# Own buffers for PSUM copies, a last norm updated on one engine, and attention heads scored in pairs, in a two-block fp32 network on one Trainium2 core

## The chip, the cores and the metric

The kernel runs on one core of a Trainium2 chip. The metric is the device time of one execution in microseconds; lower is better.

## The reference

All data are fp32; the sequence is 512 tokens of width 1024. Cut to what matters here:

```python
def first_block(x, mem, ...):                       # two layers
    for layer in range(2):
        x = x + 0.5 * swiglu_ffn(rms_norm(x, g1), w_gu, w_down)          # d_ff 2816
        h = rms_norm(x, mix_norm)
        x = x + (even_mixer(h) if layer % 2 == 0 else odd_mixer(h))
        x = x + memory_cross_attention(rms_norm(x, gx), rms_norm(mem, gm), ...)
        x = x + 0.5 * swiglu_ffn(rms_norm(x, g2), w_gu, w_down)
# even_mixer: 8 banded heads (with sinks) + 8 stick-breaking heads, head size 64
# odd_mixer:  16 heads, three dilated windows merged into one score bias
# second block: index scores of 8 heads of 64 -> top-k mask, a gated recurrence,
#   16 attention heads of 64 under that mask, a merge with gates, then
x = x + rms_norm(h @ w_att_out, out_gain)           # its norm is the "last norm" below
x = x + swiglu_ffn(rms_norm(x, g3), w_gu, w_down)   # last feed-forward block
x = rms_norm(x, g4)
```

## The kernel before

Activations stand with features on the 128 partitions and the 512 tokens along the free axis, as eight blocks `X[0..7]`. Every fp32 operand is split into a high and a low part, and each product is three matmuls: high by high, high by low, low by high (`mm3`, L312 to L314). GH and GL are the split, gain-scaled inputs of the next stage; `block_done` makes them for one block (GH on ScalarE L580, GL on VectorE L581) and adds its squares for the next norm.

A feed-forward block computes its up products as seven half-size products instead of eight (`unit`). The weights of a product are combined, cast (L427, ScalarE) and reduced by the high part (L428, VectorE). Products collect in PSUM banks x, y and z. Three times in a unit a bank's content is kept for a later sum while the bank goes on collecting: `keep` (L477) copies it on ScalarE into a slot of the common pool of 38 (L184). The products need combined inputs of block k and block k+4 too, which `pair_done` (L398 to L406) makes, mostly on VectorE.

A head of the mixers (`head`, L911 to L977) takes three PSUM banks (two in the even mixer), writes 12 score matmuls over 64 rows (L927), adds the bias and takes the maximum (L931, VectorE), exponentiates with sums (L940, ScalarE), normalises (L951, GpSimd), transposes on TensorE (L962), copies out of PSUM in two parts (`evac`, L851 ScalarE and L852 VectorE) and multiplies by the values (L975 to L977). It is a generator: `drive` steps every active head once a tick and starts new heads and "fills" (projections, output products, gates) as lists of ticks written by hand say. Head h uses rows 0 to 63 of the array if h is even, 64 to 127 if odd. The index scores of the second block use the same row halves with `mm3`.

The last norm sits in the function that ends the second block's merge. It works in two halves of 256 tokens: `update` multiplies each of the eight blocks by the factor R (L1671), adds it to the residual (L1672) and calls `block_done`. The factor comes from sums of squares over the partitions on TensorE (L545), a reciprocal root on VectorE and ScalarE (L527 to L537), transposes back (L558) and a copy (L561). A tile scheduler places every instruction in its engine's queue, by when its inputs and buffers are there in its own estimate, so an edit can move instructions that it does not touch.

Of the kernel before, what the change touches and what calls it, by code (L numbers as in the profile page):

```python
# [114 lines left out]
class Slot:  # L115
# [12 lines left out]
    @property  # L128
    def f(self):
        return self._get(F32)  # L130
# [44 lines left out]
class Net:  # L175
    def __init__(self, ctx, tc, a):
        self.ctx, self.tc, self.nc, self.a = ctx, tc, tc.nc, a
        pool = lambda name, bufs, **k: ctx.enter_context(tc.tile_pool(name=name, bufs=bufs, **k))
        self.cp = pool("const", 1)
        self.wp = pool("weights", 1)  # L180
        self.tp = pool("temps", 2)
        self.sp = pool("small", 4)
        self.ps = pool("psum", 8, space=bass.MemoryType.PSUM)
        self.room = ctx.enter_context(tc.tile_pool(name="slots", bufs=38, reuse_waits="tile"))  # L184
        self.live = self.peak = 0
        self.listed = False
        self.n = 0
        self.scope = None
        self.phase("mix")
        self.setup()  # L190
# [240 lines left out]
    def unit(self, load, B, done):  # L431
# [42 lines left out]
        def keep(b, name):  # L474
            def go():
                s = kept[name] = self.get()
                nc.scalar.copy(s.f, banks[b])  # L477
            return go

        def out(which, b, name=None):  # L480
            def go():
                s = kept.pop(name, None)
                done(which, banks[b], s and s.f)
                if s:
                    self.put(s)
            return go
# [86 lines left out]

    def block_done(self, b, c=slice(0, S), apart=1):
# [335 lines left out]

    def head(self, lay, q, k, r0, bias, v, pair, second, sink=None, gap=1):  # L911


        nc = self.nc
        mm = nc.tensor.matmul
        rows = slice(r0, r0 + 64)
        sb = [self.bank() for _ in range(lay["n"])]
        pb = self.get(lay["n"])
        mx, nm, den, rd = (self.small(NT, t, 6) for t in ("mx", "nm", "den", "rd"))
        seen = set()  # L920
# [24 lines left out]
        for _ in range(gap - 1):  # L945
            yield
        nc.vector.reciprocal(rd, den)
# [38 lines left out]
    def even_mixer(self, rms, w, wout):  # L986
# [28 lines left out]

        def a_head(h):
            p = h // 2
            if h % 2 == 0:
                st["pa", p] = []
            bt = self.vbias(a["c_bias_a"][h], 256)  # L1020
            yield from self.head(self.LAY_A, st["q", p], st["k", h // 4], (h % 2) * 64,
                                 lambda i, wd: bt.f[:, 256 - wd:256],
                                 lambda j: self.vslice(st["v"], j, 128 * (h // 4) + (64 if h % 2 == 0 else 0)),
                                 st["pa", p], h % 2 == 1, sink=sinks[:, h:h + 1], gap=2)
            self.put(bt)
            if h % 2 == 1:
                OH[p], OL[p] = self.finish_pair(st["pa", p][0])
                self.put(*st["q", p])
            if h % 4 == 3:
                self.put(*st["k", h // 4])  # L1030

# [26 lines left out]
        def b_head(h):  # L1058
# [10 lines left out]
        B = lambda h: lambda: b_head(h)  # L1069
        A = lambda h: lambda: a_head(h)  # L1070
        f = lambda g, *x: lambda: g(*x)
# [10 lines left out]
            ([f(proj_b, 0, 3)], [B(5), A(0)]),  # L1082
            ([f(proj_b, 1, 3)], [A(1)]),
            ([f(proj_q, 1)], [B(6), B(7)]),
            ([], []),
            ([], []),
            ([], [A(2)]),
            ([], [A(3)]),
            ([outs[0]], [A(4)]),
            ([], [A(5)]),  # L1090
            ([outs[1]], [A(6)]),
            ([], [A(7)]),
            ([outs[2]], []),
# [92 lines left out]
    def odd_mixer(self, rms, w, wout):  # L1186
# [20 lines left out]

        def head(h):
            p = h // 2
            if h % 2 == 0:  # L1210
                st["po", p] = []
            bt = self.vbias(a["c_bias_o"][h], 512)
            yield from self.head(self.LAY_C, st[0, p], st[1, p], (h % 2) * 64,
                                 lambda i, wd: bt.f[:, 512 - wd:512],
                                 lambda j: self.vslice(st["v", p // 2], j, (p % 2) * 192 + (h % 2) * 64),
                                 st["po", p], h % 2 == 1, gap=2)
            self.put(bt)
            if h % 2 == 1:
                OH[p], OL[p] = self.finish_pair(st["po", p][0])
                self.put(*st[0, p], *st[1, p])  # L1220

        outs = self.out_units(wout, OH, OL, range(ND))
        H = lambda h: lambda: head(h)
# [271 lines left out]
    def index_scores(self, st, W, i):  # L1495
# [5 lines left out]
        if i == 0:  # L1501
# [3 lines left out]
            return  # L1505
        for h in range(8):
            if h == 4:
                yield
            ps = self.bank()[:, :wd]
            rows = slice((h % 2) * 64, (h % 2) * 64 + 64)  # L1510
            t = slice(i * P, (i + 1) * P)
            qh, ql = iq[h // 2]
            self.mm3(ps, qh.r[rows, t], ql.r[rows, t], ik[0].r[rows, :wd], ik[1].r[rows, :wd], True, True)
            rl = self.scratch()[:, :wd]
            nc.scalar.activation(rl, ps, AF.Relu)
            wc = self.iw[:, i * 8 + h:i * 8 + h + 1]
            if h == 0:
                nc.vector.tensor_scalar(o, rl, wc, None, OP.mult)
            else:
                nc.vector.scalar_tensor_tensor(o, rl, wc, o, OP.mult, OP.add)  # L1520
        nc.vector.tensor_add(o[:, wd - P:], o[:, wd - P:], self.caus)
# [114 lines left out]
    def out_norm(self, w, XH, XL, gname):  # L1636
# [152 lines left out]
    def second(self, out):  # L1789
# [95 lines left out]

        def head(h):
            p, g = h // 2, h // 4
            if h % 2 == 0:
                st["po", p] = []
            yield from self.head(self.LAY_C, Q[p], K[g], (h % 2) * 64, bias,  # L1890
                                 lambda j: self.vslice(V[g // 2], j, 128 * (g % 2) + (64 if h % 2 == 0 else 0)),
                                 st["po", p], h % 2 == 1, gap=2)
            if h % 2 == 1:
                OH[p], OL[p] = self.finish_pair(st["po", p][0])
                self.put(*Q[p])
            if h % 4 == 3:
                self.put(*K[g])
# [23 lines left out]

        H = lambda h: lambda: head(h)
        B = lambda b: lambda: merge_b(b)
# [3 lines left out]
        for h in range(16):  # L1927
            x = [q(h // 4 + 1)] if h % 4 == 0 and h < 12 else [G(h // 2)] if h % 2 else []
            ticks.append((x, [H(h)]))
        self.drive(ticks + [([B(0)], []), ([B(1)], [])])  # L1930
# [108 lines left out]
```

## Time and profile before

| | |
|---|---|
| three runs | 3272.19, 3276.24, 3276.51 us, median 3276.24 |
| the profiled execution | 3273.41 us, span of its instructions 3271.6 us |
| TensorE, VectorE, ScalarE, GpSimd busy | 3179.1, 2245.2, 1611.8, 372.0 us |
| granted clock of TensorE, mean over the span | 0.988 |

Device times compare whole runs; the profile shows where one execution spent its span. The 1.8 us between the profiled time and its span lie around the instructions.

### The profile page before, as it was taken

To read this page: it belongs to the slowest core of one execution; us is meant where nothing else is said; L and a number is where in the kernel's file an instruction comes from. 1 tells how busy PE (TensorE), PEld (TensorE's weight loads), DVE (VectorE), ACT (ScalarE), POOL (GpSimd) and SP (SyncE) were. 2 spreads that over 40 slices of the span, in tenths; PEclk is the share of its full clock that TensorE was granted. 3 is DMA by queue.
4 is the path that set the end of the run, shared out by engine and by line. 5 is a ranking of instruction groups with operands and counts; after the bars stand their busy time and mean duration, and the time that the engine had idled before them with its cause. 6 is when DMAs were issued, how large, how long until landed. Compare 5 with 4: busy or idle time off the path is not lost. (4 is left out here: it accounts for less than half of the span.)

```text
span 3271.6 us, 51295 instructions
## 1 busy us (share of the span) xinstructions
PE 3179.1 (97%) x20612; PEld 2863.6 (88%) x20612; DVE 2245.2 (69%) x3384; ACT 1611.8 (49%) x2687; POOL 372.0 (11%) x593
## 2 busy tenths in 40 slices
PE   7999999999999999999999999999998999989998
PEld 6999888898899989999998988999876888879887
DVE  8877656656777697865666457776689455477765
ACT  6544455555444364434555554444485366354444
POOL 1000122201000010001122010000322132210001
PEclk9999999999999999999999999999999999989999
DMA  4332211322233323322223322332322322413322
GB/s 157 101 104 84 86 57 52 123 92 86 84 103 101 98 94 105 97 83 88 85 80 114 104 84 73 109 101 73 107 65 88 106 65 72 155 39 104 104 90 65
DMA packets 104335, 300.82 MB, mean 92 GB/s; under 512 B 13856, under 2 KB 17440, under 8 KB 104096
## 3 DMA queue, kind: packets, MB, share of 16 engines
q1 hardware_dynamic: 94464, 287.74, 27.3%
q10 hardware_dynamic: 9632, 9.80, 1.0%
q8 instruction: 161, 2.64, 0.3%
q14 instruction: 78, 0.64, 0.1%
HBM read 291.21 MB, written 6.29 MB: 91 GB/s over the span
## 5 line engine op out<-in xcount | busy, mean ns | idle before, releaser
L312 PE MATMUL bank<-slot,whi 128*128 128x256 f32 (+1 forms) x2768 | 913.0, 331 | 18.5 <-ACT slot L477 11.3
L313 PE MATMUL bank<-slot,whi 128*128 128x256 f32 (+1 forms) x2768 | 910.5, 329 | 0.4 <-DVE slot L518 0.4
L314 PE MATMUL bank<-slot,wlo 128*128 128x256 f32 (+1 forms) x2768 | 910.4, 329 | 0.0
L427 ACT CAST whi<-fq 128x1024 fp32r<-128x1024 f32 x350 | 366.5, 1048 | 548.4 <-PE bank L313 461.8
L306 ACT CAST whi<-raw 128x1024 fp32r<-128x1024 f32 (+3 forms) x363 | 345.5, 953 | 523.7 <-PE bank L313 318.8
L312 PEld LDWEIGHTS bank<-slot,whi 128*128 128x128 f32 x2768 | 521.6, 189 | 75.7 <-ACT slot L477 15.8
L314 PEld LDWEIGHTS bank<-slot,wlo 128*128 128x128 f32 x2768 | 522.9, 189 | 51.5
L313 PEld LDWEIGHTS bank<-slot,whi 128*128 128x128 f32 x2768 | 521.5, 188 | 52.2 <-DVE slot L518 1.5
L312 PE MATMUL bank<-gh,whi 128*128 128x256 f32 (+1 forms) x1712 | 539.9, 316 | 22.2 <-ACT whi L352 8.5
L307 DVE TENSOR_TENSOR wlo<-raw,whi 128x1024 fp32r<-128x1024 f32 (+3 forms) x363 | 407.0, 1122 | 214.5 <-ACT whi L306 213.6
L314 PE MATMUL bank<-gh,wlo 128*128 128x256 f32 (+1 forms) x1712 | 536.4, 313 | 4.2 <-DVE wlo L353 2.8
L313 PE MATMUL bank<-gl,whi 128*128 128x256 f32 (+1 forms) x1712 | 537.3, 314 | 2.8 <-DVE gl L581 2.8
L428 DVE TENSOR_TENSOR wlo<-fq,whi 128x1024 fp32r<-128x1024 f32 x350 | 427.2, 1222 | 156.5 <-ACT whi L427 156.1
L312 PEld LDWEIGHTS bank<-gh,whi 128*128 128x128 f32 x1712 | 326.3, 191 | 49.9 <-ACT whi L427 9.7
L314 PEld LDWEIGHTS bank<-gh,wlo 128*128 128x128 f32 x1712 | 326.9, 191 | 26.0 <-DVE wlo L353 3.5
L313 PEld LDWEIGHTS bank<-gl,whi 128*128 128x128 f32 x1712 | 326.8, 191 | 26.0 <-DVE gl L581 4.3
L788 PE MATMUL bank<-whi,gh 128*128 128x256 f32 (+1 forms) x1056 | 301.8, 286 | 0.0
L789 PE MATMUL bank<-wlo,gh 128*128 128x256 f32 (+1 forms) x1056 | 298.9, 283 | 1.0 <-DVE wlo L307 0.9
L790 PE MATMUL bank<-whi,gl 128*128 128x256 f32 (+1 forms) x1056 | 298.9, 283 | 1.0 <-DVE gl L581 0.8
L172 POOL TENSOR_TENSOR sqacc<-sqacc,slot 128x512 f32<-128x512 f32 x62 | 98.3, 1585 | 924.8 <-ACT slot L168 884.3
L788 PEld LDWEIGHTS bank<-whi,gh 128*128 128x128 f32 x1056 | 199.8, 189 | 1.9 <-DVE slot L855 0.3
L789 PEld LDWEIGHTS bank<-wlo,gh 128*128 128x128 f32 x1056 | 199.9, 189 | 1.8 <-DVE wlo L307 1.6
(320 smaller groups left out, 4731.2 us busy)
## 6 DMA issues: line engine op xcount, KB each, us to landing
fq<-in_ffn_w_gu_dram SPq DMA_DIRECT2D x160, 512.0 KB, 3.3
raw<-in_ffn_w_down_dram SPq DMA_DIRECT2D x96, 384.0 KB, 3.0
raw<-in_w_in_dram SPq DMA_DIRECT2D x46, 512.0 KB, 3.4
raw<-in_xa_w_kv_dram SPq DMA_DIRECT2D x32, 512.0 KB, 3.4
raw<-in_od_w_in_dram SPq DMA_DIRECT2D x24, 512.0 KB, 3.8
raw<-in_w_ffn_down_dram SPq DMA_DIRECT2D x22, 512.0 KB, 3.5
fq<-in_w_ffn_gate_dram SPq DMA_DIRECT2D x40, 256.0 KB, 2.8
fq<-in_w_ffn_up_dram SPq DMA_DIRECT2D x40, 256.0 KB, 3.1
```

The costliest lines, as they stand in the source:

```text
L172: self.net.nc.gpsimd.tensor_add(self.parts[0], self.parts[0], sq)
L306: nc.scalar.copy(hi[:, :n], raw[:, :n])
L307: nc.vector.tensor_sub(lo[:, :n], raw[:, :n], hi[:, :n].bitcast(F32))
L312: mm(ps, wh, xh, start=start, stop=False, **k)
L313: mm(ps, wh, xl, start=False, stop=False, **k)
L314: mm(ps, wl, xh, start=False, stop=stop, **k)
L427: self.nc.scalar.copy(hi[:, :n], t[:, :n])
L428: self.nc.vector.tensor_sub(lo[:, :n], t[:, :n], hi[:, :n].bitcast(F32))
L788: mm(o, XH[k][:, t], wh, start=first, stop=False, skip_group_check=True)
L789: mm(o, XH[k][:, t], wl, start=False, stop=False, skip_group_check=True)
L790: mm(o, XL[k][:, t], wh, start=False, stop=last, skip_group_check=True)
```

## The change

It makes four edits. The common pool has 36 slots and not 38, and `keep` copies into two buffers of its own (`kept`). In the last norm all eight multiplications of a half are on VectorE (four were on GpSimd), and the combined inputs of all four pairs are made behind the last block of the second half, instead of as soon as both blocks of a pair are there. In the mixers and the second block, two heads with opposite row halves become one generator `heads`, whose 24 score matmuls alternate between the halves; the rest of each head follows as before, the second head's stages being a tick later than the first's from the normalisation on, and a pair starts every second tick. The index scores alternate in the same way.

```diff
-        self.room = ctx.enter_context(tc.tile_pool(name="slots", bufs=38, reuse_waits="tile"))
+        self.room = ctx.enter_context(tc.tile_pool(name="slots", bufs=36, reuse_waits="tile"))
...
-                s = kept[name] = self.get()
-                nc.scalar.copy(s.f, banks[b])
+                kept[name] = self.tp.tile([P, 512], F32, name=self.uid("kept"), tag="kept", bufs=2)
+                nc.scalar.copy(kept[name], banks[b])
...
-            if self.pairs is not None and (b + 4) % ND in self.there:
+            if pairs and self.pairs is not None and (b + 4) % ND in self.there:
                 self.pair_done(b % 4)
...
+    def heads(self, lay, q, k, biases, values, pair, sinks=(None, None)):
+        mm = self.nc.tensor.matmul
+        sb = [[], []]
         order = sorted(range(NT), key=lambda i: (lay["Q"][i][0], lay["Q"][i][1]))
         for i in order:
             b, off, w, k0 = lay["Q"][i]
-            o = sb[b][:, off:off + w]
+            new = b == len(sb[0])
+            if new:
+                for x in sb:
+                    x.append(self.bank())
             qs, ks = slice(i * P, (i + 1) * P), slice(k0, k0 + w)
             for z, (A, B) in enumerate(((0, 0), (0, 1), (1, 0))):
-                mm(o, q[A].r[rows, qs], k[B].r[rows, ks], start=z == 0 and b not in seen, stop=z == 2, skip_group_check=True)
-            seen.add(b)
+                for x in range(2):
+                    rows = slice(64 * x, 64 * x + 64)
+                    mm(sb[x][b][:, off:off + w], q[A].r[rows, qs], k[B].r[rows, ks], start=z == 0 and new, stop=z == 2,
+                       skip_group_check=True)
+        one, two = (self.head(lay, order, sb[x], biases[x], values[x], pair, x == 1, sinks[x]) for x in range(2))
+        next(one)
+        next(two)
+        yield
+        next(one)
+        yield
+        next(one)
+        next(two)
+        yield
+        next(one, None)
+        next(two)
+        yield
+        next(two, None)
...
-        ticks += [([fills[h]] if h in fills else [], [H(h)]) for h in range(16)]
+        ticks += [([fills[h]] if h in fills else [], [] if h % 2 else [H(h // 2)]) for h in range(16)]
...
-        for h in range(8):
-            if h == 4:
+        for p in range(4):
+            if p == 2:
                 yield
...
+            for z, (A, B) in enumerate(((0, 0), (0, 1), (1, 0))):
+                for x in range(2):
+                    rows = slice(64 * x, 64 * x + 64)
+                    mm(ps[x], iq[p][A].r[rows, t], ik[B].r[rows, :wd], start=z == 0, stop=z == 2)
...
-                (nc.gpsimd if b % 2 else nc.vector).tensor_mul(m, m, R)
+                nc.vector.tensor_mul(m, m, R)
                 nc.vector.scalar_tensor_tensor(self.X[b][:, c], m, self.col(gname, b), self.X[b][:, c], OP.mult, OP.add)
-                self.block_done(b, c, 4)
+                self.block_done(b, c, 4, False)
+            if z:
+                for k in range(4):
+                    self.pair_done(k)
```

Three places show what the scheduler makes of it. On TensorE, in the odd mixer, the 12 score matmuls of one head stood together, between a projection and transposes; one bank after the other:

```order
L927 MATMUL bank_16247<-slot_15754,slot_15842 128x512
L927 MATMUL bank_16247<-slot_15755,slot_15842 128x512
L927 MATMUL bank_16247<-slot_15754,slot_15843 128x512
L927 MATMUL bank_16248<-slot_15754,slot_15842 128x384
L927 MATMUL bank_16248<-slot_15755,slot_15842 128x384
L927 MATMUL bank_16248<-slot_15754,slot_15843 128x384
L927 MATMUL bank_16248<-slot_15754,slot_15842 128x128
```

Now, at the same place, the end of a pair's run (the scores are at L925, the transposes of an earlier stage at L859), with the banks 16257 and 16271 of one head and 16258 and 16272 of the other:

```order
L925 MATMUL bank_16257<-slot_15755,slot_15842 128x128
L925 MATMUL bank_16258<-slot_15755,slot_15842 128x128
L925 MATMUL bank_16257<-slot_15754,slot_15843 128x128
L925 MATMUL bank_16258<-slot_15754,slot_15843 128x128
L925 MATMUL bank_16271<-slot_15754,slot_15842 128x256
L925 MATMUL bank_16272<-slot_15754,slot_15842 128x256
L925 MATMUL bank_16271<-slot_15755,slot_15842 128x256
L925 MATMUL bank_16272<-slot_15755,slot_15842 128x256
L925 MATMUL bank_16271<-slot_15754,slot_15843 128x256
L925 MATMUL bank_16272<-slot_15754,slot_15843 128x256
L859 MATMUL bank_16311<-ident,slot_16141 128x128 x2
L859 MATMUL bank_16311<-ident,slot_16143 128x128 x2
```

Each head's matmul is followed by the other head's; the second head's run, which stood some 85 rows further on, is gone from there.

On ScalarE, at the start of the second feed-forward block (the casts L427 are weights, L517 inputs of the down product, `gu` the gate), before:

```order
L427 CAST whi_8532<-fq_8374 128x1024
L635 ACT_TABLE_LOAD
L635 ACTIVATE gu_8514<-gu_8514 128x512 [waits DVE_49]
L427 CAST whi_8563<-fq_8366 128x1024 [waits PE_49]
L635 ACTIVATE gu_8523<-gu_8523 128x512 [waits DVE_49]
L427 CAST whi_8595<-fq_8364 128x1024 [waits PE_49]
L517 CAST slot_8519<-gu_8514 128x512 [waits DVE_49]
L427 CAST whi_8625<-fq_8368 128x1024 [waits PE_49,Activation_49]
L517 CAST slot_8528<-gu_8523 128x512 [waits DVE_49]
L477 COPY slot_8561<-bank_8536 128x512
L427 CAST whi_8691<-fq_8683 128x1024 [waits PE_49]
```

and now (`kept` is the copy's own buffer):

```order
L427 CAST whi_8532<-fq_8374 128x1024
L632 ACT_TABLE_LOAD
L632 ACTIVATE gu_8514<-gu_8514 128x512 [waits DVE_49]
L477 COPY kept_8561<-bank_8536 128x512 [waits PE_49]
L427 CAST whi_8563<-fq_8366 128x1024
L427 CAST whi_8595<-fq_8364 128x1024 [waits PE_49]
L632 ACTIVATE gu_8523<-gu_8523 128x512 [waits DVE_49]
L514 CAST slot_8519<-gu_8514 128x512 [waits DVE_49]
L427 CAST whi_8625<-fq_8368 128x1024 [waits PE_49,Activation_49]
L514 CAST slot_8528<-gu_8523 128x512 [waits DVE_49]
```

The first copy moved six rows up, ahead of three casts of weights. On TensorE the product that goes on in that bank (product 6) moved ahead of product 5.

On VectorE, in the second half of the last norm (x0 to x7 are the residual blocks, gl0 to gl7 the low parts of the next inputs, L400 to L403 and L518 the combined inputs), before:

```order
L1672 SCALAR_TENSOR_TENSOR x2_83<-slot_4720_28812,pv_108,x2_83 128x256
L400 TENSOR_TENSOR slot_4789_29222<-slot_4788_29220 128x256
L581 SCALAR_TENSOR_TENSOR gl5_94<-x5_92,pv_108,gh5_93 128x256
L581 SCALAR_TENSOR_TENSOR gl2_85<-x2_83,pv_108,gh2_84 128x256
L401 SCALAR_TENSOR_TENSOR slot_4789_29222<-x4_89,pv_108,slot_4788_29220 128x256
L402 SCALAR_TENSOR_TENSOR slot_4790_29223<-x4_89,pv_108,slot_4789_29222 128x256
L1672 SCALAR_TENSOR_TENSOR x6_95<-slot_4748_28964,pv_108,x6_95 128x256
L403 SCALAR_TENSOR_TENSOR slot_4790_29223<-x4_89,pv_108,slot_4790_29223 128x256
L518 TENSOR_TENSOR slot_4792_29229<-slot_4789_29222,slot_4791_29228 128x512
L581 SCALAR_TENSOR_TENSOR gl6_97<-x6_95,pv_108,gh6_96 128x256
L518 TENSOR_TENSOR slot_4794_29233<-slot_4790_29223,slot_4793_29232 128x512
L1672 SCALAR_TENSOR_TENSOR x3_86<-slot_4726_28848,pv_108,x3_86 128x256
```

and now:

```order
L1685 TENSOR_TENSOR slot_4748_28964<-slot_4748_28964,R_4785_29205 128x256
L578 SCALAR_TENSOR_TENSOR gl5_94<-x5_92,pv_108,gh5_93 128x256
L578 SCALAR_TENSOR_TENSOR gl2_85<-x2_83,pv_108,gh2_84 128x256
L1686 SCALAR_TENSOR_TENSOR x6_95<-slot_4748_28964,pv_108,x6_95 128x256
L1685 TENSOR_TENSOR slot_4726_28848<-slot_4726_28848,R_4785_29205 128x256
L1685 TENSOR_TENSOR slot_4750_28992<-slot_4750_28992,R_4785_29205 128x256
L578 SCALAR_TENSOR_TENSOR gl6_97<-x6_95,pv_108,gh6_96 128x256
L1686 SCALAR_TENSOR_TENSOR x3_86<-slot_4726_28848,pv_108,x3_86 128x256
L1686 SCALAR_TENSOR_TENSOR x7_98<-slot_4750_28992,pv_108,x7_98 128x256
L578 SCALAR_TENSOR_TENSOR gl3_88<-x3_86,pv_108,gh3_87 128x256
L578 SCALAR_TENSOR_TENSOR gl7_100<-x7_98,pv_108,gh7_99 128x256
L400 TENSOR_TENSOR slot_4795_29260<-slot_4794_29258 128x256
```

The multiplications of blocks 1, 3, 5 and 7 came to VectorE (slot_4726 and slot_4750 belong to x3 and x7), and the rows of the combined inputs left their places between the blocks; they begin behind the low part of x7.

## Rows read from the trace of the kernel before

In a timeline a row is: start, duration (us), engine, line, operation, output<-input, array, shape, count; in brackets the idle time ahead and what ended it.

**Rows 1.** The page, part 1: busy us, share of the span, instructions.

```profile
PE 3179.1 (97%) x20612; PEld 2863.6 (88%) x20612; DVE 2245.2 (69%) x3384; ACT 1611.8 (49%) x2687; POOL 372.0 (11%) x593
```

**Rows 2.** Windows, odd mixer: length, busy PE, PEld, DVE, ACT, POOL, PEclk, DMA.

```profile
1660.00:1720.00 60.00, 60.00 (x453) 56.90 (x452) 39.64 (x97) 35.53 (x85) 12.36 (x34) 1.00 0.27 89
```

**Rows 3.** Groups by line, whole span: busy us, mean ns, idle before.

```profile
L927 PE MATMUL bank<-slot,slot 64*128 64x128 f32 (+3 forms) x480 | 84.6, 321 | 0.3 <-ACT slot L854 0.3
```

**Rows 4.** Timeline of PE, a head of the even and one of the odd mixer.

```profile
521.84 1.67 PE L927 MATMUL bank<-slot,slot 64*128 64x128 f32 x12
...
1611.14 2.17 PE L927 MATMUL bank<-slot,slot 64*128 64x512 f32 x12
1613.25 0.39 PE L788 MATMUL bank<-whi,gh 128*128 128x256 f32 x1
```

**Rows 5.** Timeline of PE, index scores of four heads, first and behind the last.

```profile
2391.41 0.46 PE L312 MATMUL bank<-slot,slot 64*128 64x384 f32 x2
...
2392.68 0.50 PE L312 MATMUL bank<-gh,whi 128*128 128x512 f32 x1
```

**Rows 6.** Groups by line, window 1580 to 1750 us, odd mixer.

```profile
L931 DVE CUSTOM_DVE_ANT_0 slot<-bank,slot 128x384 f32<-128x384 f32 (+3 forms) x59 | 25.7, 483 | 5.9 <-DMA slot<-in_c_bias_o_dram 3.4 <-PE bank L927 2.5
L852 DVE TENSOR_TENSOR slot<-bank,slot 128x512 fp32r<-128x512 f32 (+1 forms) x48 | 26.8, 606 | 13.3 <-ACT slot L851 13.1
```

**Rows 7.** Waits of PE, by releasing line: us in total, times, longest.

```profile
PE bank L312 <- ACT slot L477: 11.3, 9, 2.1
PE bank L312 <- ACT whi L427: 8.0, 8, 1.1
```

**Rows 8.** Timeline of ACT, start of the second feed-forward block.

```profile
838.53 0.63 ACT L635 ACTIVATE gu<-gu 128x512 f32<-128x512 f32 x1
...
843.11 1.04 ACT L427 CAST whi<-fq 128x1024 fp32r<-128x1024 f32 x1 [1.02 <-PE bank L313]
...
844.58 0.58 ACT L477 COPY slot<-bank 128x512 f32<-128x512 f32 x1
```

**Rows 9.** Timeline of PE, the same place.

```profile
845.21 0.39 PE L312 MATMUL bank<-slot,whi 128*128 128x256 f32 x1 [2.08 <-ACT slot L477]
...
849.36 0.39 PE L312 MATMUL bank<-gh,whi 128*128 128x256 f32 x1 [1.01 <-ACT whi L427]
```

**Rows 10.** Windows, last norm.

```profile
2868.00:2880.00 12.00, 6.53 (x31) 5.66 (x30) 10.76 (x25) 5.35 (x13) 3.49 (x5) 0.65 0.30 87
...
2900.00:2912.00 12.00, 12.00 (x83) 12.00 (x83) 8.82 (x17) 8.04 (x13) 0.00 (x0) 0.77 0.00 1
```

**Rows 11.** Timeline of PE, last norm, the five longest stops.

```profile
2870.63 0.50 PE L312 MATMUL bank<-gh,whi 128*128 128x256 f32 x2 [2.33 <-ACT gh L580]
...
2873.75 0.58 PE L313 MATMUL bank<-gl,whi 128*128 128x256 f32 x1 [2.28 <-DVE gl L581]
...
2893.27 0.38 PE L312 MATMUL bank<-gh,whi 128*128 128x256 f32 x1 [1.70 <-ACT gh L580]
...
2899.57 1.86 PE L545 MATMUL bank<-ones,sqacc 128*128 128x1 f32 x8 [2.75 <-POOL sqacc L172]
...
2921.35 1.08 PE L558 MATMUL bank<-ident,nry 128*128 128x128 f32 x4 [4.45 <-DVE nry L537]
```

**Rows 12.** Timeline of DVE, last norm.

```profile
2867.35 1.83 DVE L1671 TENSOR_TENSOR slot<-slot,R 128x256 f32<-128x256 f32 x2
...
2876.16 0.75 DVE L1671 TENSOR_TENSOR slot<-slot,R 128x256 f32<-128x256 f32 x2
...
2880.54 0.48 DVE L581 SCALAR_TENSOR_TENSOR gl<-x,pv,gh 128x256 fp32r<-128x256 f32 x1 [0.58 <-ACT gh L580]
...
2885.06 1.31 DVE L1671 TENSOR_TENSOR slot<-slot,R 128x256 f32<-128x256 f32 x2 [4.04 <-ACT R L561]
...
2900.45 0.87 DVE L581 SCALAR_TENSOR_TENSOR gl<-x,pv,gh 128x256 fp32r<-128x256 f32 x2
```

**Rows 13.** Timeline of POOL, last norm.

```profile
2867.99 3.50 POOL L1671 TENSOR_TENSOR slot<-slot,R 128x256 f32<-128x256 f32 x4
```

More of the change, by code (lines that the diff above doesn't have):

```diff
@@ L481, in go @@
             def go():
[L482 to L485, printed above, removed]
+                done(which, banks[b], kept.pop(name, None))
             return go
@@ L572, in norm_of, with block_done @@
         self.there = set()
-    def block_done(self, b, c=slice(0, S), apart=1):
+    def block_done(self, b, c=slice(0, S), apart=1, pairs=True):
         nc = self.nc
@@ L909, in pt_slots @@
         return s, [s[0].r, s[1].r, s[4].r[:, :256]], [s[2].r, s[3].r, s[4].r[:, 256:]]
[L911 to L920, printed above, removed]
+    def heads(self, lay, q, k, biases, values, pair, sinks=(None, None)):
+        mm = self.nc.tensor.matmul
+        sb = [[], []]
         order = sorted(range(NT), key=lambda i: (lay["Q"][i][0], lay["Q"][i][1]))
@@ L923, in head @@
             b, off, w, k0 = lay["Q"][i]
-            o = sb[b][:, off:off + w]
+            new = b == len(sb[0])
+            if new:
+                for x in sb:
+                    x.append(self.bank())
             qs, ks = slice(i * P, (i + 1) * P), slice(k0, k0 + w)
             for z, (A, B) in enumerate(((0, 0), (0, 1), (1, 0))):
-                mm(o, q[A].r[rows, qs], k[B].r[rows, ks], start=z == 0 and b not in seen, stop=z == 2, skip_group_check=True)
-            seen.add(b)
+                for x in range(2):
[15 more added lines that the diff above has]
+        next(two, None)
+    def head(self, lay, order, sb, bias, v, pair, second, sink):
+        nc = self.nc
+        mm = nc.tensor.matmul
+        pb = self.get(lay["n"])
+        mx, nm, den, rd = (self.small(NT, t, 6) for t in ("mx", "nm", "den", "rd"))
         for i in order:
@@ L944, in head @@
             nc.vector.tensor_add(den, den, es)
-        for _ in range(gap - 1):
-            yield
+        yield
         nc.vector.reciprocal(rd, den)
@@ L1014, in proj_kv, with a_heads @@
             self.put(tm)
[L1016 to L1024, printed above, removed]
-            self.put(bt)
[L1026 to L1030, printed above, removed]
+        def a_heads(p):
+            st["pa", p] = []
+            bt = [self.vbias(a["c_bias_a"][2 * p + x], 256) for x in range(2)]
+            yield from self.heads(self.LAY_A, st["q", p], st["k", p // 2],
+                                  [lambda i, wd, t=t: t.f[:, 256 - wd:256] for t in bt],
+                                  [lambda j, c=c: self.vslice(st["v"], j, 128 * (p // 2) + c) for c in (64, 0)],
+                                  st["pa", p], [sinks[:, 2 * p + x:2 * p + x + 1] for x in range(2)])
+            self.put(bt)
+            OH[p], OL[p] = self.finish_pair(st["pa", p][0])
+            self.put(*st["q", p])
+            if p % 2 == 1:
+                self.put(*st["k", p // 2])
         def feat_b(which, p):
@@ L1069, in even_mixer @@
         B = lambda h: lambda: b_head(h)
-        A = lambda h: lambda: a_head(h)
+        A = lambda p: lambda: a_heads(p)
         f = lambda g, *x: lambda: g(*x)
@@ L1206, in proj, with heads @@
             self.put(tm)
[L1208 to L1216, printed above, removed]
+        def heads(p):
+            st["po", p] = []
+            bt = [self.vbias(a["c_bias_o"][2 * p + x], 512) for x in range(2)]
+            yield from self.heads(self.LAY_C, st[0, p], st[1, p], [lambda i, wd, t=t: t.f[:, 512 - wd:512] for t in bt],
+                                  [lambda j, c=c: self.vslice(st["v", p // 2], j, (p % 2) * 192 + c) for c in (0, 64)],
+                                  st["po", p])
             self.put(bt)
-            if h % 2 == 1:
-                OH[p], OL[p] = self.finish_pair(st["po", p][0])
-                self.put(*st[0, p], *st[1, p])
+            OH[p], OL[p] = self.finish_pair(st["po", p][0])
+            self.put(*st[0, p], *st[1, p])
         outs = self.out_units(wout, OH, OL, range(ND))
-        H = lambda h: lambda: head(h)
+        H = lambda p: lambda: heads(p)
         f = lambda *x: lambda: proj(*x)
@@ L1884, in bias, with heads @@
             return W[b].f[:, off:off + wd]
[L1886 to L1896, printed above, removed]
+        def heads(p):
+            g = p // 2
+            st["po", p] = []
+            yield from self.heads(self.LAY_C, Q[p], K[g], (bias, bias),
+                                  [lambda j, c=c: self.vslice(V[g // 2], j, 128 * (g % 2) + c) for c in (64, 0)], st["po", p])
+            OH[p], OL[p] = self.finish_pair(st["po", p][0])
+            self.put(*Q[p])
+            if p % 2 == 1:
                 self.put(*K[g])
@@ L1920, in merge_b @@
             yield from self.out_unit(a["w_att_out_2"][0], b, OH, OL, range(ND), finish)
-        H = lambda h: lambda: head(h)
+        H = lambda p: lambda: heads(p)
         B = lambda b: lambda: merge_b(b)
```

40 lines of the change are left out of this document (20 added, 20 removed).

## The prediction

> **What bounds the kernel now.** I read the busy times first: TensorE is busy for 3179.1 us, 97% of the span [rows 1]. So a change pays only if it takes matmul time off TensorE or removes one of its few stops; a change that speeds up VectorE, ScalarE or GpSimd does nothing by itself. The windows came second: in the odd mixer, between 1660 and 1720 us, TensorE fills all 60.00 us, VectorE 39.64 and ScalarE 35.53 [rows 2]. The other two have about a third of their time free there, which matters for the paired heads. Third came the waits of TensorE by the line that released it, and fourth the timeline of the two places where it stops in series: the start of a feed-forward block and the last norm of the second block. The measurement tells a difference from none at about 0.2%, 6.5 us here.
>
> **Part 1, the heads.** A head's scores are 12 matmuls which contract over 64 rows, half of the array; there are 480 of them, 40 heads [rows 3]. In the 512-wide layout (odd mixer and second block, 32 heads) a run of 12 starts at 1611.14 and the next matmul at 1613.25: 2.11 us [rows 4]. In the even mixer a run takes 1.67 us (8 heads) [rows 4]. The change issues the runs of two heads that lie in opposite row halves as one run of 24 that alternates between them. Does the array run the halves together? The index scores show it: 64-row matmuls of 384 columns, four heads in all, 12 matmuls, from 2391.41 to 2392.68, 1.27 us [rows 5]. A run of 12 on one half takes 2.11 us for 3840 columns [rows 4], 0.55 ns a column; 12 times 384 columns would at that rate be 2.53 us. The measured 1.27 is half of it, and the records stand as pairs (x2) with one start: halves overlap fully. So a pair costs what one head costs. 16 pairs of the wide kind each save 2.11 us: 33.8. Four even pairs save 4 x 1.67 = 6.7 [rows 4]. Three pairs do not come out as one run in the order (one even pair falls into pieces of 3, 3, 4, 4 and 10, one odd pair is 1 + 23, the last pair of the second block 2, 1, 1 and 20); for these I take off 2.0. Sum 38.5 us.
>
> What it costs: a pair takes six PSUM banks at once, where a head took three, out of eight. They come free when VectorE has reduced them, four reductions of 0.483 us a head, 1.93 us [rows 6], so 3.86 us for the pair. The transposes that stand right behind the pair in TensorE's new order need a bank each. The bounds are 0 (TensorE always finds the two remaining banks enough) and one further head's reductions at each pair, 20 x 1.93 = 39. VectorE has a third of its time free [rows 2], so over a whole pair it catches up, and only the burst behind the scores waits. In the new order the banks come round after some 1.0 to 1.6 us of TensorE work in five of eight odd pairs, 0.7 to 1.2 us short each, and little elsewhere. I take 8 us, nearer to 0 than to 39. The longer softmax chain (recip, normalise, transposes one tick later) lies beside projections and gates. Net for the heads: **-30 us**, own bounds -38 to 0; likely -22 to -37.
>
> **The index scores** get the same alternation, but stood as three matmuls of one head and then three of the other, and the trace already shows them overlapped [rows 5]: 0 us. Two slots fewer in the common pool: a pair now takes the slots of two heads at once, but the three copies of a feed-forward unit no longer take any; 0, with the 8 us above as the bound in the mixers.
>
> [...]
>
> **Part 2, PSUM copies with own buffers.** At a feed-forward start ScalarE stands for a cast of weights (843.11) which waits 1.02 us for TensorE, and only behind it comes the copy of product 1 (844.58) [rows 8]. TensorE needs that copy to reuse the bank: it stops for 2.08 us at 845.21, and again 1.01 us at 849.36 because the weight cast is late in turn [rows 9]. Over the whole span the two kinds of stop are 11.3 us in 9 places and 8.0 in 8 [rows 7], 19.3 in all. In the new order the copy stands directly behind the first Silu, ahead of the casts (see the order of ScalarE above), so TensorE's product 6 finds its bank free, and the copy comes some 5 us sooner (near 839.1, where the first Silu of this start ends, instead of 844.58). Left over: the copy into a buffer which waits for VectorE's use of product 1 (the third of a unit, only two buffers); behind it on ScalarE stands the next cast, and it has a whole product to be ready. Bounds: 0 gain, if the casts are late for another reason, to 19.3. I take **-15 us**, since at one of the starts a shorter wait for weights may stay.
>
> **Part 3, the last norm.** From 2868 to 2880 us TensorE is busy for 6.53 of 12 us, at a granted clock of 0.65, and from 2900 to 2912 at 0.77 [rows 10]. Five stops carry 13.5 us (2.33 + 2.28 + 1.70 + 2.75 + 4.45) [rows 11]. VectorE is what they wait for: a multiplication of 256 columns there takes 0.37 us when GpSimd is quiet (0.75 for two, at 2876.16) and 0.91 while GpSimd multiplies too (1.83 for two, at 2867.35) [rows 12], and GpSimd needs 3.50 us for four [rows 13]. The second half begins only at 2885.06, after 4.04 us of idle VectorE, and its last low part comes at 2901 [rows 12]. In the new order all eight multiplications are on VectorE, each block costing 0.37 + 0.43 + 0.43 = 1.23 us (the low part is 0.87 for two [rows 12], the update of the residual is the same operation), 9.9 us a half, and the combined inputs (four small operations and two splits for each pair) stand behind the second half. The first half, which starts at 2867.35 and has a weight split of about 1.2 us in its midst, then ends near 2878.5 instead of 2881 [rows 12]; the factor of the second half is there by then, as its transposes stand earlier in TensorE's order, and the second half ends near 2889 instead of 2901. The next factor, for which TensorE waited till 2921.35 [rows 11], would come near 2905. What is late next: the last pair's split, near 2914, for which product 6 or 5 waits. The gain is 16 us, **-16**, bounds -8 (the pairs eat half) and -20.
>
> **Sum.** 3273.4 (the profiled execution, 2.8 under the median of 3276.2) - 30 - 15 - 16 = 3212; half of the 2.8 added, 3214.
>
> **Rivals.**
> *Banks given back.* The overlap of the halves is there, but TensorE waits at most pairs for the reductions: one head's 1.93 us at each of 20 is 39 us, all of the 38.5. For it: six of eight banks, and the burst of 3.86 us. Against it: VectorE a third free. Heads give 0 to -10: 3273 - 5 - 31 = about 3238. Chance 0.17. The Trainium skill, "TensorEngine Tiling (Array Packing)", Performance Considerations, names PSUM evacuation as what may become the limit once row tiling has sped TensorE up; whether it does here the rows above leave open.
> *VectorE becomes the bound of the last norm.* It takes GpSimd's multiplications, and the combined inputs come last; then the stage gains some 4 us and not 16: 3226. Chance 0.07. Against it: GpSimd's multiplications make VectorE's own slower than taking them over [rows 12].
> *The kept copies change nothing*, because the casts set the pace: 3214 + 15 = 3229. Chance 0.03.
> *Slower than before.* TensorE waits at each pair for both heads' reductions and two of the copies behind the transposes (0.606 each [rows 6]): 3.86 + 1.21 = 5.07 us, 20 pairs 101 us, less 38.5 and 31: 3273 + 32 = 3305. It decides from a wait of (38.5 + 31) / 20 = 3.5 us a pair. Against it: the copies are no part of what the next scores need. Chance 0.03.
> *The index scores gain as well*, were their halves apart before: some 7 us (their six runs at about 1.2 us again), 3207. Chance 0.01, as the pairs in [rows 5] speak against it.
>
> **How the numbers follow.** The forecast has 0.69: 3214, with its own range of 3200 to 3228. Rival 1 reaches to 3243, the slower rival is left out, and the low end takes all bounds of the heads and feed-forward gains (3273 - 38 - 19 - 20 = 3196). Range 3196 to 3241. Faster by over 0.2%: 0.95; within 0.2%: 0.02 (between the first rival and the slower one); slower: 0.03.
>
> **What would show it.** Right: head runs of about 2.0 to 2.2 us with 24 matmuls and records in pairs; waits on L477 and L427 below 5 us together; in the last norm no stop over 3 us and the factor of the next norm before 2908 in old time. Wrong: new waits of TensorE on the reductions at the transposes behind a pair, of over 1 us at most pairs; a stop in the last norm at the split of the last pair; a half clock in the mixer.

## The result, and the profile after

The changed kernel took 3241.53 us (median of four runs, 3231.84 to 3244.69), the kernel before 3276.16 (also of four); the ratio is 0.9892, 95% interval 0.9868 to 0.9916, so it is some 35 us faster. The forecast was 3214: the direction was right, the gain a little over half of the forecast. The median stands half a microsecond above the upper end of the range, 3241, inside the spread of the four runs, and near where the first rival (banks given back, 3238) had put it.

The page of the profiled execution (3244.69 us, the slowest of the four) gives one line in answer to [rows 1]. TensorE is 27 us less busy, and the span is 28.7 us shorter, so nearly nothing of its stops went in sum.

```profile
PE 3152.3 (97%) x20612; PEld 2839.3 (88%) x20612; DVE 2237.6 (69%) x3392; ACT 1607.5 (50%) x2687; POOL 366.9 (11%) x585
```

The waits of TensorE by releasing line (total us, times, longest) show why. The two lines of [rows 7], 11.3 and 8.0 us, have all but gone. The waits for the heads' reductions (L949; L931 before, where no such wait stands) are new.

```profile
PE bank L925 <- DVE mx L949: 6.2, 4, 2.5
...
PE bank L859 <- DVE mx L949: 1.7, 2, 1.1
...
PE bank L312 <- DVE mx L949: 1.2, 1, 1.2
...
PE bank L312 <- ACT whi L427: 1.0, 1, 1.0
...
PE bank L312 <- ACT kept L477: 0.7, 1, 0.7
```

**The overlap is there.** The timeline of TensorE has a pair in the second block: 24 matmuls from 2648.49 to the next at 2650.61, 2.12 us, where one head took 2.11 [rows 4]. In the even mixer 24 take the 1.67 us that 12 took [rows 4]. The index scores of four heads take 1.27 us (2387.64 to 2388.91), to the hundredth what they took before [rows 5].

```profile
501.96 1.67 PE L925 MATMUL bank<-slot,slot 64*128 64x128 f32 x24
505.85 0.33 PE L1179 MATMUL bank<-slot,tri 128*128 128x128 f32 x1 [2.22 <-POOL slot L1161]
...
1566.13 1.79 PE L925 MATMUL bank<-slot,slot 64*128 64x512 f32 x18
1570.38 1.30 PE L925 MATMUL bank<-slot,slot 64*128 64x256 f32 x6 [2.46 <-DVE mx L949]
...
2387.64 1.34 PE L1525 MATMUL bank<-slot,slot 64*128 64x384 f32 x12
2388.91 0.50 PE L312 MATMUL bank<-gh,whi 128*128 128x512 f32 x1
...
2648.49 2.19 PE L925 MATMUL bank<-slot,slot 64*128 64x512 f32 x24
2650.61 0.50 PE L312 MATMUL bank<-gh,whi 128*128 128x512 f32 x1
```

**But a pair waits for itself.** In the odd mixer the first pair stops inside its run: 18 matmuls, 2.46 us of nothing, then the last six. VectorE at that time (below) works off two weight splits and a sum of squares with a small operation behind it, which waits for GpSimd, before it comes to the pair's first reduction at 1569.63; that ends at 1570.32, and the six begin at 1570.38. By these times the third banks of a pair are banks that its own first head's scores still hold.

```profile
1566.14 2.45 DVE L307 TENSOR_TENSOR wlo<-raw,whi 128x1024 fp32r<-128x1024 f32 x2 [1.38 <-ACT whi L306]
1568.50 0.68 DVE L818 TENSOR_REDUCE hss<-slot 128x8 f32<-128x512 f32 x1
1569.51 0.16 DVE L821 SCALAR_TENSOR_TENSOR hy<-nry 128x4 f32<-128x4 f32 x1 [0.33 <-POOL hss L824]
1569.63 0.69 DVE L949 CUSTOM_DVE_ANT_0 slot<-bank,slot 128x512 f32<-128x512 f32 x1
```

That is not the cause at every pair. At five of the eight pairs of the odd mixer VectorE stands idle ahead of the first reduction (1.06, 0.49, 0.35, 1.95 and 2.14 us) until the transfer of the score bias has landed, which the reduction reads too. The transfer is sent for about when the pair starts and takes 3.0 us in the median. Four stops of TensorE, 4.8 of the 10.1 us of waits on the reductions, stand behind these (at 1618.80, 1644.13, 1678.34 and 1742.48). The shorter of stop and idle time at each adds up to 3.0 us, the most that biases sent for earlier would give back there by these rows, the clock aside. That was not tried.

```profile
1618.05 0.69 DVE L949 CUSTOM_DVE_ANT_0 slot<-bank,slot 128x512 f32<-128x512 f32 x1 [1.06 <-DMA slot<-in_c_bias_o_dram]
...
1741.73 0.69 DVE L949 CUSTOM_DVE_ANT_0 slot<-bank,slot 128x512 f32<-128x512 f32 x1 [2.14 <-DMA slot<-in_c_bias_o_dram]
```

```profile
1742.48 0.50 PE L312 MATMUL bank<-slot,whi 128*128 128x512 f32 x1 [1.24 <-DVE mx L949]
```

A window over 200 us of the odd mixer (as in [rows 2]) gives the sum: TensorE busy 185.24, granted clock 0.97.

```profile
1547.00:1747.00 200.00, 185.24 (x1399) 173.03 (x1398) 115.19 (x298) 101.37 (x253) 40.58 (x107) 0.97 0.25 77
```

**Feed-forward start.** On ScalarE the copy stands at 836.95, directly behind the first Silu as the order said, and both stops of [rows 9] are gone from this start.

```profile
836.41 0.64 ACT L632 ACTIVATE gu<-gu 128x512 f32<-128x512 f32 x1
836.95 0.57 ACT L477 COPY kept<-bank 128x512 f32<-128x512 f32 x1
```

**Last norm.** The transposes L555 begin at 2853.23 for the first factor (2865.77 before) and at 2898.96 for the next norm's (2921.35 [rows 11]). The stage between is 9.85 us shorter; in old time the next norm's factor comes at 2911.5, behind the 2908 that the prediction had set as its sign of being right. Then TensorE stops for 2.66 us at the split of the last pair (L514). The window below them has the granted clock, 0.72, of the stretch with the sums of squares (L542).

```profile
2853.23 0.38 PE L555 MATMUL bank<-ident,nry 128*128 128x128 f32 x2
...
2887.66 5.40 PE L542 MATMUL bank<-ones,slot 128*128 128x1 f32 x32
...
2898.96 0.60 PE L555 MATMUL bank<-ident,nry 128*128 128x128 f32 x4
...
2906.46 0.58 PE L312 MATMUL bank<-slot,whi 128*128 128x256 f32 x1 [2.66 <-ACT slot L514]
```

```profile
2887.00:2899.00 12.00, 11.32 (x72) 11.13 (x71) 6.71 (x15) 4.92 (x9) 0.00 (x0) 0.72 0.09 21
```

### The profile page after: what moved, and what is told of

Read it like the earlier page. It is cut to its first block, busy times and chain, and to the rows that moved or that the text cites. A ratio compares the mean times of both kernels' runs of the same rounds, so it can differ in the third digit from the quotient of the medians.

```text
span 3242.9 us, 51346 instructions
## 1 busy us (share of the span) xinstructions
PE 3152.3 (97%) x20612; PEld 2839.3 (88%) x20612; DVE 2237.6 (69%) x3392; ACT 1607.5 (50%) x2687; POOL 366.9 (11%) x585
## 5 line engine op out<-in xcount | busy, mean ns | idle before, releaser
L427 ACT CAST whi<-fq 128x1024 fp32r<-128x1024 f32 x350 | 365.7, 1048 | 505.1 <-PE bank L313 403.9
```

What stands on the lines that cost most here:

```text
L427: self.nc.scalar.copy(hi[:, :n], t[:, :n])
```

## The experiments

Ratios are to the kernel before on the same chip, with 95% intervals; the us beside them are the distance of the ratio from 1, times 3272.

### Each part alone

Own buffers alone:

```diff
-                s = kept[name] = self.get()
+                kept[name] = self.tp.tile([P, 512], F32, ..., tag="kept", bufs=2)   # and 36 slots
```

> The kernel before with the own buffers of the PSUM copies alone (36 slots, two kept buffers). In the profile of the changed kernel the five feed-forward blocks came earlier by 6.4, 4.3, 2.9, 3.2 and 9.9 us. Theory: all of it is this edit, so about 3276 - 27 = 3249. Rival: the 9.9 us of the last block belong to the edit of the last norm ahead of it, so 3276 - 17 = 3259 and no more.

Measured: 0.9907 (0.9893 to 0.9920), -30 us. The theory holds. The waits on L477 and L427 are 1.9 and 0.8 us. The profiled executions are 28.2 us apart. Of these 16.6 are the waits, and 6.2 are other stops: of its span of 3243.4 us TensorE stands idle for 69.7, where before it stood for 92.5. The largest of the others are at the factors of the norms (6.0 us before, 2.2 now) and at the last block's down product (3.3, 0.9). The remaining 5.4 us are time that TensorE is less busy; the mean granted clock is 0.988 in both, so it does not explain them, and they stay open.

```profile
PE 3173.7 (98%) x20612; PEld 2862.4 (88%) x20612; DVE 2239.4 (69%) x3384; ACT 1609.5 (50%) x2687; POOL 370.2 (11%) x593
```

The last norm alone, and of it the multiplications alone (the first pair of lines of this diff):

```diff
-                (nc.gpsimd if b % 2 else nc.vector).tensor_mul(m, m, R)
+                nc.vector.tensor_mul(m, m, R)
-                self.block_done(b, c, 4)
+                self.block_done(b, c, 4, False)          # and pair_done(0..3) behind half 1
```

> The kernel before with the edit of the last norm alone (multiplications on VectorE, combined inputs behind the second half). Theory: the factor of the next norm comes 10 us sooner, and the stop at the split of the last pair takes 3 to 4 back: 3276 - 6 = 3270. Rival: the last feed-forward block gains from it as well, 3276 - 16 = 3260.

> The kernel before with the multiplications of the last norm all on VectorE and nothing else; the combined inputs stay between the blocks. Theory: the multiplications on GpSimd delayed the blocks, and this half of the edit brings 5 to 7 of the 9 us: ratio 0.998. Rival: the gain is that of the combined inputs behind the last block: 1 to 2 us, ratio 0.9995.

Measured: 0.9973 (0.9962 to 0.9984), -9 us, for both, and 0.9979 (0.9970 to 0.9988), -7 us, for the multiplications. The interval of the first holds its theory's 6 us and not its rival's 16; the second agrees with its theory. So the multiplications on GpSimd were the delay; moving the combined inputs adds little, within what these intervals can tell.

The pairs alone (38 slots, index scores as before; `heads` as in the change, and for instance):

```diff
...
-        ticks += [([fills[h]] if h in fills else [], [H(h)]) for h in range(16)]
+        ticks += [([fills[h]] if h in fills else [], [] if h % 2 else [H(h // 2)]) for h in range(16)]
...
```

> The kernel before with the paired heads alone (38 slots, index scores and everything else as before). Theory: what the overlap of the row halves saves on TensorE is given back as waits for PSUM banks, for both heads' chains and as half clock: even mixer +4.5, odd mixer +6, second block -10, so 3276 within 5. Rival: the pairs are held back by the pool with two slots fewer, which is not so here: then 20 us or more are gained, 3256 or less.

Measured: 0.9981 (0.9973 to 0.9990), -6 us of the 38.5 that the overlap saves: just past the 5 us that the theory allowed, and far from the rival's 20. The pool's two slots are not the reason: with 38 slots the odd mixer's waits on the reductions are nearly the same (5.8 us in 4 places at the scores, 6.2 in the changed kernel).

All but the pairs, that is, the first two parts together:

> The changed kernel without its pairs: own buffers and the last norm's edit, heads and index scores as before. Theory: as the pairs give back what they save, this is as fast as the changed kernel, 3276 - 27 - 6 = 3243. Rival (the pairs gain and the other two edits give less than their stages show): 3255 or more.

Measured: 0.9897 (0.9884 to 0.9911), -34 us: as fast as the changed kernel (0.9892). Beside the other two parts the pairs bring nothing that can be told: in the profiled executions the changed kernel's TensorE is 19.7 us less busy than this one's and stands idle 24.8 us longer. In its 200 us of the odd mixer (the same place in the program) TensorE hardly stops, and its clock stays at 1.00:

```profile
1541.00:1741.00 200.00, 199.88 (x1460) 186.70 (x1458) 118.93 (x303) 105.79 (x267) 42.33 (x111) 1.00 0.24 77
```

Against it the changed kernel loses 14.6 us of busy time and, at a clock of 0.97, some 5.6 more (0.03 x 185), 20 in all; eight pairs save 8 x 2.11 = 16.9. Of the 14.6, 10.1 are waits on the reductions; most of the rest are waits for other operations of VectorE that empty banks (the longest 2.65 us, for a copy out of PSUM at L852).

### Where the pairs pay

Pairs in the second block alone, then in the odd mixer and the second block (the other heads one by one, with the two other parts in both):

> Own buffers, the last norm's edit, index scores as before, and pairs in the second block alone; the heads of the even and the odd mixer one by one as before. Theory: the pairs gain 10 us in the second block and lose in the two mixers: 3240 - 10 = 3230, ratio 0.987. Rival: once the other edits are in, the pairs of the second block give nothing either: 3240.

> Own buffers, the last norm's edit, index scores as before, pairs in the odd mixer and in the second block; the heads of the even mixer one by one. Theory: pairs in the odd mixer lose 6 us against single heads: ratio to before 0.989 to 0.990, where the same without them stood at 0.9875. Rival: the odd mixer's loss in the changed kernel came with the pool of 36 slots or with the state that the even mixer left, and the ratio is 0.987 or less.

The edit of the first run in the odd mixer, against the changed kernel:

```diff
-            yield from self.heads(self.LAY_C, st[0, p], st[1, p], ...                    # odd mixer
+            yield from self.head_one(self.LAY_C, st[0, p], st[1, p], (h % 2) * 64, ...   # the head of before
```

Measured: 0.9875 (0.9858 to 0.9892), -41 us, and 0.9899 (0.9882 to 0.9916), -33 us. Both theories hold by their points, though the two intervals overlap and the first reaches its rival's 0.989. Pairs in the second block alone are the fastest version measured, ahead of the changed kernel by 0.17%, which these times do not tell from none.

The stages of the profiled executions do tell the two places apart. From the first score matmul of the odd mixer to the sums of squares of the next norm (L545, L542) it is 240.8 to 244.0 us in the six kernels with single heads there (before, own buffers, last norm, multiplications, all but the pairs, pairs in the second block alone). It is 247.2, 248.9 and 249.9 in the three with pairs as in the change. From the first score matmul of the second block to the factor of the last norm it is 250.4 to 252.5 in the five kernels with single heads and 239.7 to 241.1 in the four with pairs. So against the kernel before the pairs alone give back 20 us in the odd mixer (16.9 saved, 3.2 longer) and 6 in the second block (16.9 saved, 11.2 shorter). In the even mixer none of the 6.7 shows: from the norm ahead of it to the factor of the second feed-forward block it is 448.1 us with the pairs alone and 445.3 to 448.2 with single heads. Together that is the 32 us that are missing. Rows of the second block, before and pairs alone:

```profile
2614.83 2.18 PE L927 MATMUL bank<-slot,slot 64*128 64x512 f32 x12 [0.34 <-ACT slot L854]
...
2865.77 0.38 PE L558 MATMUL bank<-ident,nry 128*128 128x128 f32 x2
```

```profile
2619.62 2.52 PE L928 MATMUL bank<-slot,slot 64*128 64x512 f32 x24 [0.34 <-ACT slot L854]
...
2859.32 0.38 PE L558 MATMUL bank<-ident,nry 128*128 128x128 f32 x2
```

### Is it the reductions?

Each head's reductions done twice, in the pairs and, as the control, in the kernel before:

```diff
+            for _ in range(2):
-            nc.vector.tensor_tensor_reduce(pb[b].f[:, off:off + w], sb[b][:, off:off + w], ...)
+                nc.vector.tensor_tensor_reduce(pb[b].f[:, off:off + w], sb[b][:, off:off + w], ...)
```

> The paired heads alone, with each head's four reductions of its scores (VectorE) done twice, to the same result. Theory: the pairs' banks are held by the reductions, and TensorE waits for them; twice the reductions hold the last bank up to 3.9 us longer at each of 20 pairs: 3267 + 30 to 60, with most of it in the odd mixer. Rival: what the pairs gave back is lost cover of other chains, not the reductions' time: +10 or less.

> The kernel before with the same doubling of the reductions, as the control: VectorE has the same 77 us more to do, but a head holds three banks alone. Theory: under +15. Rival (VectorE's total work is what counts, not the banks that a pair holds): as much more as the doubled pairs.

Measured: 1.0066 (1.0050 to 1.0082), 28 us over the pairs alone, and 1.0081 (1.0063 to 1.0099), 26 us over before. By the totals the control took the theory's side away: the same work costs single heads as much. The places differ, though. By the stages as above, the odd mixer is 268.0 us with doubled pairs, 20.8 longer than with the pairs alone, and 248.3 with doubled single heads, 4.3 longer than before. In the second block it is the other way round: 6.0 us longer with pairs, 10.8 with single heads. The odd mixer, doubled pairs and then doubled single heads:

```profile
1579.22 1.79 PE L928 MATMUL bank<-slot,slot 64*128 64x512 f32 x18
...
1847.26 0.95 PE L545 MATMUL bank<-ones,sqacc 128*128 128x1 f32 x8
```

```profile
1583.89 2.19 PE L927 MATMUL bank<-slot,slot 64*128 64x512 f32 x12
...
1832.20 0.95 PE L545 MATMUL bank<-ones,sqacc 128*128 128x1 f32 x8
```

In the odd mixer the waits on the reductions are these for the doubled pairs (20.8 us; 9.0 in the pairs alone):

```profile
PE bank L928 <- DVE mx L953: 11.5, 5, 4.0
PE bank L312 <- DVE mx L953: 2.7, 2, 1.5
PE bank L862 <- DVE mx L953: 2.6, 2, 2.0
PE bank L996 <- DVE mx L953: 2.4, 4, 0.7
PE bank L788 <- DVE mx L953: 1.6, 1, 1.6
```

and these for the doubled single heads (1.8 us):

```profile
PE bank L963 <- DVE mx L932: 1.1, 3, 0.6
PE bank L788 <- DVE mx L932: 0.7, 1, 0.7
```

So in the odd mixer longer reductions hold up the pairs nearly five times as much as single heads. That the whole loss of the pairs is this wait is not shown.

A pair in two parts, four banks in one tick and two in the next:

```diff
+        scores([i for i in order if lay["Q"][i][0] < late])
         next(one)
         next(two)
         yield
+        scores([i for i in order if lay["Q"][i][0] == late])
+        next(one)
+        next(two)
         next(one)
```

> As the run with pairs in the odd mixer and the second block, but a pair writes its first two banks a head (18 matmuls) in one tick and the third (6 matmuls) in the next, so that it takes four banks at once and two later. Theory: the odd mixer's stops are waits for the reductions to free banks, so most of the 10 us of them go, less 0.2 us for each second entry into 64-row work: 5 us or more faster than the unsplit run. Rival: the stops come from the longer chain of two heads, and a part that starts a tick later makes them longer: no faster, or slower by 5 us.

Measured: 0.9955 (0.9941 to 0.9969), 18 us slower than the unsplit run; the rival holds, and by more than its 5 us. The waits on the reductions in the odd mixer fall to 3.9 us, as the theory had it, but a new one takes their place: exponentials and normalisation begin a tick later, and the transposes wait for GpSimd. The odd mixer, then the second block, where the unsplit run waits 0.8 us for it:

```profile
PE bank L989 <- POOL slot L978: 8.0, 3, 4.0
PE bank L785 <- DVE mx L959: 3.0, 2, 2.7
...
PE bank L989 <- POOL slot L978: 13.6, 4, 5.0
```

The second head's scores copied out by ScalarE first:

```diff
+        if second:
+            for b in range(lay["n"]):
+                nc.scalar.copy(pb[b].f[:, :lay["qused"][b]], sb[b][:, :lay["qused"][b]])
+            src = [x.f for x in pb]
```

> As the run with pairs in the odd mixer and the second block (ratio 0.9899), but the second head's scores are first copied out of PSUM by ScalarE (0.58 us for 512 columns), and VectorE reduces them from there; the chain of the softmax keeps its ticks. Theory: the pair's banks come free after VectorE's 1.93 us for the first head instead of 3.86 for both, so most of the odd mixer's 10 us of waits on the reductions and its half clock go: ratio 0.987 or less. Rival: the reductions are late because of what stands ahead of them on VectorE, and ScalarE's copies stand behind casts in turn: 0.989 to 0.991.

Measured: 0.9894 (0.9875 to 0.9912), no different from 0.9899; the rival holds. The first pair stops as long as ever, since its bank waits for the first head's first reduction, and that stands behind the same four instructions on VectorE:

```profile
1564.84 1.78 PE L925 MATMUL bank<-slot,slot 64*128 64x512 f32 x18
1569.09 1.69 PE L925 MATMUL bank<-slot,slot 64*128 64x256 f32 x6 [2.47 <-DVE mx L954]
```

### Is the alternation needed?

```diff
-            for z, (A, B) in enumerate(((0, 0), (0, 1), (1, 0))):
-                for x in range(2):
+        for x in range(2):
+            for i in order:          # all 12 of one head, then the other's
```

> The paired heads alone, but a pair's 24 score matmuls stand as 12 of the first head and then 12 of the second, not alternating. Theory A: the array runs opposite row halves side by side even when their matmuls do not alternate (as the index scores of before show for 3 and 3); then runs take about 2.1 to 2.5 us and the time is that of the alternating pairs, 3267 within 6. Theory B: overlap needs the alternation; then runs take 4.2 us, 40 us of TensorE time come back, less the waits that they hide (10 to 13 us in the odd mixer): 3267 + 10 to 30 = 3277 to 3297.

Measured: 1.0025 (1.0017 to 1.0034), 14 us over the alternating pairs. Theory A falls. B's time holds (3277 to 3297; the ratio makes it 3280), its run of 4.2 us doesn't: in the second block 24 take 3.63 us (2665.68 to 2669.31), so a part of the second head still runs beside the first.

```profile
2665.68 3.70 PE L927 MATMUL bank<-slot,slot 64*128 64x512 f32 x24
2669.31 0.50 PE L312 MATMUL bank<-gh,whi 128*128 128x512 f32 x1
```

## Why the prediction was right and wrong

**The heads: wrong.** The saving of 38.5 us stands (2.12 and 1.67 us for 24 matmuls). The step that failed is "over a whole pair it catches up, and only the burst behind the scores waits. ... I take 8 us". About 32 were given back: the first rival's sum, though not by its mechanism. It had one head's reductions waited for at every pair. In fact the odd mixer gives back 20 us for eight pairs: 10.1 in stops of up to 2.5 us at the reductions, some 4 in waits for other VectorE operations that empty banks, and the half clock in which TensorE goes on behind such stops, which I had not priced. The second block waits little (by line 1.6, 0.8, 0.7 and 0.3 us) and keeps 11 of its 16.9. VectorE's free third [rows 2] was no cover. The reductions are late by what stands ahead of them in its queue or by the bias that VectorE itself waits for, not by how busy it is on average. In the even mixer the stop of 2.22 us behind the first pair waits for GpSimd's part of the stick-breaking heads, not for a bank: it looks as if the scores that moved had covered that chain. That was argued from the rows and not tried. Of the prediction's signs of being wrong the half clock in the mixer came; waits at the transposes behind a pair came at one pair only (1.14 and 0.60 us).

The Trainium skill's warning ("TensorEngine Tiling (Array Packing)", Performance Considerations: evacuation of PSUM may become the limit) came true in the odd mixer, with 9.0 us of waits on the reductions for the pairs alone, and not in the second block, where no wait on them stands.

**The index scores: right.** 1.27 us before and after. In the profiles of the changed kernel, of the run without pairs and of two others this region was 4 us longer, also where the index scores were as before; it is not the edit.

**Own buffers: right mechanism, half the size.** -15 was the term, -30 was measured. The wait itself fell from 19.3 to 2.7 us, 16.6, close to the term. The upper bound of 19.3 held only the two releasers' stops, and not the 6.2 us of other stops that went with them, nor the 5.4 us of busy time whose cause is open.

**The last norm: right mechanism, too large.** -16 was the term; the factor of the next norm came 9.9 us sooner, and -9 was measured. The second half ends where the walk said (its last low part ends at 2878.35, 2890.9 in old time, forecast 2889). What did not shrink is the stretch from there to the next factor, 20.6 us: 32 small sums of squares take 5.40 us, with the clock at 0.72, and five small operations of the reciprocal root take from 2893.10 to 2897.36, since operations on weights and on combined inputs stand between them on VectorE. Before, it was 20.0 us (from 2901.32 to 2921.35 [rows 11, 12]); the forecast allowed 16 (2889 to 2905) and gave no reason. Its "VectorE is what they wait for" is more than [rows 11] say: they name VectorE at two of the five stops, 6.7 of 13.5 us, and ScalarE and GpSimd at the others. The stop at the last pair's split came as named.

```profile
2877.46 0.89 DVE L578 SCALAR_TENSOR_TENSOR gl<-x,pv,gh 128x256 fp32r<-128x256 f32 x2 [0.18 <-ACT gh L577]
...
2893.10 0.16 DVE L548 TENSOR_SCALAR nv<-bank 128x4 f32<-128x4 f32 x1 [5.29 <-PE bank L542]
...
2897.20 0.16 DVE L534 TENSOR_TENSOR nry<-nry,nrt 128x4 f32<-128x4 f32 x1
```

So the sum was 61 us and the parts gave 30, 9 and 0 to 6; two terms too large and one too small. That the time still came out next to the upper end of the range is luck: own buffers gave 15 us more than their term, and the heads 24 less. What stays open: how much of the odd mixer's loss is wait and how much is clock that a wait of another length would not have cost. Open too is whether the pairs would be free with the reductions ahead of the weight splits on VectorE and the biases sent for earlier; neither was tried.

## What to carry to other kernels

Work that overlaps on the array needs its PSUM banks at one time: ask for the first bank that the second half of a run waits for, and read what stands in the queue of the engine that frees it and what that engine waits for itself (a bias still on its way, here), not that engine's busy share. Where it stands short, as in the second block, overlap pays; take it place by place. A copy that frees a bank should not stand behind casts in its engine's queue: moving it gained most of this change, 30 us where its stops had shown 19.

## What the runs showed of the hardware

Opposite row halves do not keep the program's order between them. Three matmuls of one half and then three of the other start in pairs [rows 5], in the records at most 12 ns apart; 12 and 12 overlap in part (3.63 us against 2.12 alternating). GpSimd beside VectorE slows it again: while GpSimd adds squares at 2869.11, a low part takes 1.52 us that takes 0.47 us alone.

```profile
2869.11 3.06 POOL L172 TENSOR_TENSOR sqacc<-sqacc,slot 128x512 f32<-128x512 f32 x2 [13.63 <-ACT slot L168]
```

```profile
2866.13 0.47 DVE L578 SCALAR_TENSOR_TENSOR gl<-x,pv,gh 128x256 fp32r<-128x256 f32 x1
...
2869.52 1.52 DVE L578 SCALAR_TENSOR_TENSOR gl<-x,pv,gh 128x256 fp32r<-128x256 f32 x1
```
